# A Hymba-style decoder step: the down products in Strassen's form, the FFN in two phases, and PSUM read in bank pairs

## The chip, the cores and the metric

The kernel runs on one core of a Trainium2 chip. The metric is the device time of one execution in microseconds (us). TensorE (PE) multiplies; a matmul takes a 128x128 block of weights and up to 512 columns of a right operand and accumulates in PSUM, eight banks of 512 float32 columns for each of 128 partitions. VectorE (DVE) and ScalarE (ACT) work on SBUF and PSUM, GpSimd (POOL) on small things, and SyncE (SP) issues nearly all the transfers, in the order of the program, to 16 DMA engines.

## The reference

One decoder layer over 1048 tokens (16 meta tokens, 1024 of a prompt, 8 samples), width 1024. It is a macaron: a half FFN, a mixer (an HGRN2 group and a Mamba-2 group side by side), and a second half FFN.

```python
D_FF = 2816
def swiglu(x, wg, wu, wd):
    return (jax.nn.silu(x @ wg) * (x @ wu)) @ wd

h = h + 0.5 * swiglu(rmsnorm(h, n1), w1g, w1u, w1d)
u = rmsnorm(h, nm) @ w_in
...                                  # HGRN2 and Mamba-2, both with a state
h = h + mix                          # concat(o_hg, yz) @ w_out
h = h + 0.5 * swiglu(rmsnorm(h, n2), w2g, w2u, w2d)
```

All is float32. Besides the 1032 output rows, the states of both groups and of the convolution are returned.

## The kernel before, in words

Activations lie transposed: a tile holds 128 features by T = 1048 tokens, and Q = T/4 = 262 tokens are a quarter. A float32 product is made of three matmuls (`mm3`, L129): each operand is split into a rounded high part (`nc.scalar.copy` into float32r on ScalarE, L126) and the rest (a subtraction on VectorE, L127), and high by high, high by low and low by high are summed in PSUM.

An FFN takes the 2816 hidden features in 22 blocks `f` of 128. `pair` (L300) computes gate and up of one block together as a 2x2 block product in the Strassen-Winograd form: 7 products where the plain form has 8. Its left operands are four pieces of weights and four sums of them (`sum_`, L317, on VectorE), its right operands four blocks of the normed input and four sums, already split and resident in 28 tiles. Each of the 7 products is done for two column halves c, four chunks of the inner dimension and three matmuls each: 14 steps of 12 matmuls of 262 columns. After a step, one operation reads its PSUM bank (L390 to L404); the products come in the order 1, 6, 2, 5, 7, 3, 4, where 2, 3 and 4 add to the banks of 1, 5 and 7. At the end the hidden block silu(g)·u is formed (L409) and split.

`down` (L418) multiplies by the down weights in the plain form. The 22 blocks make six groups of 3 or 4. One pair after a group is complete, its down product is done: 8 output blocks `o` by 4 quarters, 3n matmuls each into a bank of its own, then `h += 0.5·ps` on VectorE (L449). The residual h lies in DRAM in half tiles; it is loaded before and stored after each group (L439, L451). The last group goes quarter by quarter, so that the next norm or the final rows can start on finished quarters.

The order inside an FFN is written out by hand. `Steps` (L275) holds the TensorE steps; `S.before(i, fn)` puts loads, sums and splits ahead of step i. PE, DVE, ACT and SP execute exactly in the order so written. In a pair, weights are asked for 10 and 9 steps ahead, their sums are made 7 to 5 steps ahead, and their splits from 4 steps ahead, one every second step. Outside the FFNs a scheduler orders the work; it may put mixer work between the last steps of the first FFN.

PSUM has two pools of four banks: `acc` for pairs and the mixer's products, `mis` for down products, transposes and norms. SBUF has 30 large slots with the tag `u` and 8 with the tag `s`, nine half tiles `t`, eight weight pieces `r`, and six split weights `ws`.

Of the kernel before, what the change touches and what calls it, by code (L numbers as in the profile page):

```python
# [17 lines left out]
P = 128  # L18
# [46 lines left out]
class Core:  # L65
    def __init__(self, ctx, tc):
# [7 lines left out]
        self.acc = ent(tc.tile_pool(name="acc", bufs=4, space=PSUM))  # L74
# [3 lines left out]
        self.n = 0  # L78

# [15 lines left out]

    def psum(self):
        return self.acc.tile([P, 512], F32, tag="acc", name=self.uid("acc"))
# [202 lines left out]
def pair(K, S, wg, wu, f, ops, first=None):  # L300
# [7 lines left out]
    w, raw, ps, tm, gu, hid = {}, {}, {}, {}, {}, []  # L308

    def load(p, src, k0):  # L310
        raw[p] = K.raw()
        nc.sync.dma_start(raw[p].rearrange("p (k c) -> p k c", k=4), src[:, k0 : k0 + 4, fs])

    def sum_(p, x, y, op):
        if p not in raw:
            raw[p] = K.raw()
        nc.vector.tensor_tensor(raw[p], raw[x], raw[y], op)  # L317

    def split(p):
        w[p] = K.split_w(raw[p])  # L320

    loads = [lambda: load(1, wg, 0), lambda: load(7, wu, 0), lambda: load(4, wu, 4), lambda: load(2, wg, 4)]
    sums = [
        lambda: sum_(5, 7, 4, ALU.add),
        lambda: sum_(6, 5, 1, ALU.subtract),
        lambda: sum_(7, 1, 7, ALU.subtract),
        lambda: sum_(3, 2, 6, ALU.subtract),
    ]
    if first:
        order, blocks, between = first  # L330
        for fn in loads:
            fn()

        def weights():
            for fn in sums:
                fn()
            for p in ORDER[:6]:
                split(p)

        if order == "w":  # L340
            weights()
        blocks(0)
        ops[0].sums()
        for p in ORDER[:2] if order == "w" else ORDER:
            ops[0].split(p)
        if order == "x":
            weights()
        else:
            for i, p in enumerate(ORDER[2:]):
                S.before(s0 + i, lambda p=p: ops[0].split(p))  # L350
        S.before(s0 + 4, lambda: blocks(1))
        S.before(s0 + 4, ops[1].sums)
        S.before(s0 + 6, between)
        for i, p in enumerate(ORDER):
            S.before(s0 + 6 + max(0, i - 1), lambda p=p: ops[1].split(p))
        S.before(s0 + 9, lambda: split(4))
    else:
        for fn, d in zip(loads, (-10, -10, -9, -9)):
            S.before(s0 + d, fn)
        for fn, d in zip(sums, (-7, -7, -6, -5)):  # L360
            S.before(s0 + d, fn)
        for i, p in enumerate(ORDER):
            S.before(s0 + 2 * i - (4 if f > 1 else 3), lambda p=p: split(p))

    def product(p, c):
        if p in (1, 6, 5, 7):
            ps[p, c] = K.psum()[:, :Q]
        more = p in (2, 3, 4)
        if more:
            ps[p, c] = ps[{2: 1, 3: 5, 4: 7}[p], c]  # L370
        wp = w[p]
        hi, lo = ops[c].op[p]
        for k in range(4):
            K.mm3(ps[p, c], wp[:, k * P : k * P + P], wp[:, 512 + k * P : 512 + k * P + P], hi[:, k * Q : k * Q + Q], lo[:, k * Q : k * Q + Q], not more and k == 0, k == 3, more)

    def temp(n, c):
        if n not in tm:
            tm[n] = K.t(2 * Q)
        return tm[n][:, c * Q : c * Q + Q]

    def out(i, q):

        if (i, q // 2) not in gu:
            gu[i, q // 2] = K.t(2 * Q)
        return gu[i, q // 2][:, (q % 2) * Q : (q % 2) * Q + Q]

    def post(p, c):
        b = ps[p, c]
        if p == 1:
            nc.scalar.copy(temp("z", c), b)  # L390
        elif p == 6:
            nc.vector.tensor_add(temp("v", c), b, temp("z", c))
        elif p == 2:
            nc.scalar.activation(out(0, 2 * c), b, AF.Silu)  # L394
        elif p == 5:
            nc.vector.tensor_add(temp("x", c), b, temp("v", c))
        elif p == 7:
            nc.vector.tensor_add(out(1, 2 * c + 1), b, temp("x", c))
        elif p == 3:
            g = out(0, 2 * c + 1)  # L400
            nc.vector.tensor_add(g, b, temp("v", c))  # L401
            nc.scalar.activation(g, g, AF.Silu)  # L402
        else:
            nc.vector.tensor_add(out(1, 2 * c), b, temp("v", c))  # L404
            cs = slice(2 * c * Q, 2 * c * Q + 2 * Q)
            if c == 0:
                hid.extend(K.slot("s" if f % 5 else "u", T, F32R) for i in range(2))
            g, u = gu[0, c], gu[1, c]
            nc.vector.tensor_mul(g, g, u)  # L409
            K.split(g, hid[0][:, cs], hid[1][:, cs])  # L410

    for p, c in [(p, c) for ps_ in (ORDER[:6], ORDER[6:]) for c in range(2) for p in ps_] if first else [(p, c) for p in ORDER for c in range(2)]:
        S.add(lambda p=p, c=c: product(p, c), lambda p=p, c=c: post(p, c))
    return hid
# [1016 lines left out]
```

## Time and profile before

| what | value |
|---|---|
| three runs | 2208.37, 2211.03, 2211.6 us; median 2211.03 |
| profiled execution | 2207.17 us, span 2205.5 us, mean granted clock 0.975 |
| TensorE busy | 2077.0 us (94%), 16078 matmuls |
| VectorE / ScalarE busy | 1306.7 us (59%) / 745.8 us (34%) |
| DMA | 239.40 MB, 35.4% of 16 engines on SP's queue |
| first FFN | about 80 to 815 us |
| second FFN | about 1465 us to the end |

The span runs from the first to the last instruction. TensorE's busy time is the union of its matmuls, which overlap; the distance from start to start is shorter than a duration. The granted clock is the share of full speed that TensorE was given. The table of stretches gives the busy time of each engine and the number of its instructions (x) between two times, then the granted clock, the mean busy share of the DMA engines and the GB/s that they moved. The share can stand above 1.00, since packets overlap. In a group of instructions "out<-in" names tiles, and the last part gives the idle time before them and what ended most of it. In the order of time, square brackets hold the idle time of the engine before an instruction and what ended it.

### The profile page before, as it was taken

The numbers are of one execution on the slowest core, as the hardware profiler recorded it, in microseconds if no ns is written. First come the engines' busy times: TensorE is split into PE (matmuls) and PEld (weight loads), VectorE is DVE, ScalarE is ACT, GpSimd is POOL, SyncE is SP. The second block draws the span as 40 slices with busy tenths as digits, with TensorE's granted clock in tenths as the row PEclk, the third lists the DMA queues.
The fourth block names the chain that finished last, engine by engine and source line by source line (L and its number), as shares of the span: only waits on it lengthen the run. The fifth ranks groups of instructions, "written<-read, shape, count | busy, mean of one in ns | idle before, by whom it ended". The sixth has DMA issues, their size and how long they took to land.

```text
span 2205.5 us, 39636 instructions
## 1 busy us (share of the span) xinstructions
PE 2077.0 (94%) x16078; PEld 2032.7 (92%) x16078; DVE 1306.7 (59%) x2576; ACT 745.8 (34%) x1475; POOL 137.4 (6%) x175
## 2 busy tenths in 40 slices
PE   3899999999999989989999999969999999999996
PEld 3899999999999879978989988969999999999996
DVE  5655646465564586588554457876564655646465
ACT  6422313132231353464523435543131322313122
POOL 1000000000000130141011011300000000000000
PEclk9999999999999999989999999989999999999999
DMA  3425161523516521163022053221625244262542
GB/s 118 107 84 170 54 200 47 171 89 104 154 54 200 156 100 36 55 184 95 36 69 76 4 170 123 86 71 53 198 59 176 73 120 133 59 198 59 175 137 92
DMA packets 276829, 239.40 MB, mean 109 GB/s; under 512 B 18656, under 2 KB 221664, under 8 KB 276640
## 3 DMA queue, kind: packets, MB, share of 16 engines
q1 hardware_dynamic: 275832, 234.73, 35.4%
q8 instruction: 127, 2.08, 0.4%
q10 hardware_dynamic: 592, 2.10, 0.3%
q14 instruction: 54, 0.44, 0.1%
q0 software_dynamic: 224, 0.04, 0.0%
HBM read 169.81 MB, written 67.08 MB: 107 GB/s over the span
## 4 chain that ended last, share of the span: by engine, by line
PE 47%; DVE 5%; ACT 1%; issue 1%; DMA 1%; POOL 0%; SPq 0%; DVEq 0%; ACTq 0%; POOLq 0%
PE acc L134 10%; PE acc L132 10%; PE acc L133 10%; PE mis L132 4%; PE mis L133 3%; PE mis L134 3%; PE mis L1115 2%; DVE s L1129 1%; DVE u L127 1%; PE mis L1154 0%; ACT u L1247 0%; DVE ws L127 0%; DVE u L1253 0%; PE mis L1172 0%; PE mis L1210 0%
## 5 line engine op out<-in xcount | busy, mean ns | idle before, releaser
L132 PE MATMUL acc<-u,ws 128*128 128x262 f32 (+2 forms) x3392 | 1001.5, 295 | 21.3 <-ACT u L126 17.7
L133 PE MATMUL acc<-u,ws 128*128 128x262 f32 (+2 forms) x3392 | 998.5, 294 | 12.1 <-DVE u L127 11.8
L134 PE MATMUL acc<-u,ws 128*128 128x262 f32 (+2 forms) x3392 | 997.5, 294 | 0.0
L132 PEld LDWEIGHTS acc<-u,ws 128*128 128x128 f32 x3392 | 645.9, 190 | 24.3 <-ACT u L126 18.2
L133 PEld LDWEIGHTS acc<-u,ws 128*128 128x128 f32 x3392 | 647.9, 191 | 16.3 <-DVE u L127 14.5
L134 PEld LDWEIGHTS acc<-u,ws 128*128 128x128 f32 x3392 | 645.2, 190 | 0.4
L127 DVE TENSOR_TENSOR ws<-r,ws 128x512 fp32r<-128x512 f32 (+1 forms) x484 | 329.9, 685 | 241.9 <-ACT ws L126 241.3
L126 ACT CAST ws<-r 128x512 fp32r<-128x512 f32 (+1 forms) x484 | 280.6, 613 | 391.7 <-DMA r<-in_w_ffn_down_dram 256.8
L132 PE MATMUL mis<-s,ws 128*128 128x262 f32 x1024 | 293.7, 287 | 2.2 <-DVE u L449 1.3
L133 PE MATMUL mis<-s,ws 128*128 128x262 f32 x1024 | 292.4, 286 | 0.7 <-DVE s L127 0.7
L134 PE MATMUL mis<-s,ws 128*128 128x262 f32 x1024 | 292.2, 285 | 0.0
L449 DVE SCALAR_TENSOR_TENSOR t<-mis,t 128x262 f32<-128x262 f32 x320 | 132.8, 428 | 156.9 <-PE mis L134 156.4
L132 PEld LDWEIGHTS mis<-s,ws 128*128 128x128 f32 x1024 | 195.0, 190 | 3.3 <-DVE u L449 1.7
L133 PEld LDWEIGHTS mis<-s,ws 128*128 128x128 f32 x1024 | 194.9, 190 | 1.3 <-DVE s L127 1.1
L134 PEld LDWEIGHTS mis<-s,ws 128*128 128x128 f32 x1024 | 194.7, 190 | 0.0
L402 ACT ACTIVATE t<-t 128x262 f32<-128x262 f32 x88 | 37.2, 423 | 315.4 <-DVE t L401 315.4
L317 DVE TENSOR_TENSOR r<-r,r 128x512 f32<-128x512 f32 x176 | 121.4, 691 | 37.1 <-DMA r<-in_w_ffn_up_dram 35.6
L132 PE MATMUL mis<-u,ws 128*128 128x262 f32 x288 | 83.1, 289 | 6.8 <-DVE t L449 6.8
L126 ACT CAST s<-t 128x524 fp32r<-128x524 f32 x68 | 42.9, 631 | 126.7 <-DVE t L409 126.7
L133 PE MATMUL mis<-u,ws 128*128 128x262 f32 x288 | 82.6, 287 | 0.0
L134 PE MATMUL mis<-u,ws 128*128 128x262 f32 x288 | 82.6, 287 | 0.0
L394 ACT ACTIVATE t<-acc 128x262 f32<-128x262 f32 x88 | 34.3, 390 | 132.5 <-PE acc L134 132.5
(353 smaller groups left out, 2101.3 us busy)
## 6 DMA issues: line engine op xcount, KB each, us to landing
hd<-t SPq DMA_DIRECT2D x160, 262.0 KB
t<-hd SPq DMA_DIRECT2D x144, 262.0 KB
r<-in_w_ffn_gate_dram SPq DMA_DIRECT2D x88, 256.0 KB
r<-in_w_ffn_up_dram SPq DMA_DIRECT2D x88, 256.0 KB
r<-in_w_ffn_down_dram SPq DMA_DIRECT2D x64, 256.0 KB
r<-in_w_in_dram SPq DMA_DIRECT2D x56, 256.0 KB
u<-hd SPq DMA_DIRECT2D x32, 262.0 KB
r<-in_w_out_dram SPq DMA_DIRECT2D x32, 256.0 KB
```

The source lines that it names most:

```text
L126: self.nc.scalar.copy(hi, src)
L127: self.nc.vector.tensor_sub(lo, src, hi.bitcast(F32))
L132: mm(ps, whi, xhi, start=first, stop=False, skip_group_check=more)
L133: mm(ps, whi, xlo, start=False, stop=False, skip_group_check=more)
L134: mm(ps, wlo, xhi, start=False, stop=last, skip_group_check=more)
L317: nc.vector.tensor_tensor(raw[p], raw[x], raw[y], op)
L394: nc.scalar.activation(out(0, 2 * c), b, AF.Silu)
L402: nc.scalar.activation(g, g, AF.Silu)
L449: nc.vector.scalar_tensor_tensor(t, ps, 0.5, t, ALU.mult, ALU.add)
L1115: nc.tensor.matmul(ps[:, 64 * c : 64 * c + 64], kg[:, P * c : P * (c + 1)], qv[:, c, :, 1], start=True, stop=True)
L1129: nc.vector.tensor_mul(fn, fv[:, :, 0], fv[:, :, 1])
```

## The change

- `down` becomes a Strassen-Winograd product too. A unit j takes two output blocks (2j, 2j+1) and n pairs of hidden blocks: 7 products by 2 column halves, each n chunks by three matmuls, 14 steps of 3n matmuls. The weights of a unit are n·128-column pieces and their four sums, as in `pair`; both use the new `left`, with the same leads.
- The right operands of down are the four blocks of a pair of hidden blocks and four differences of them, each split. `Hidden.jobs` makes them while the next pairs run and stores each of the 7, both parts together, to DRAM.
- The FFN has two phases: first all 22 pairs, then all down units, in three groups of 3, 4 and 4 pairs of hidden blocks, four units each. `Hidden.load` loads a group's 14 operands (7 products by 2 halves, two parts each) into the large slots; they stay for its four units.
- h goes through DRAM as whole tiles, loaded by each unit four steps ahead and stored two steps after, except in the last group, which keeps it.
- PSUM: `acc` has two tiles of two banks. `Unit.both` puts the two halves of a product into one pair, and one instruction reads both (524 columns). `psum()` of the mixer hands out halves of a pair.
- The last unit goes half by half, and the next norm or the final rows start after its first half.

```diff
-        self.acc = ent(tc.tile_pool(name="acc", bufs=4, space=PSUM))
+        self.acc = ent(tc.tile_pool(name="acc", bufs=2, space=PSUM))
...
+    def psum2(self):
+        self.half = None
+        return self.acc.tile([P, 2, 512], F32, tag="acc", name=self.uid("acc"))
...
+    if at:
+        for fns, ds in zip((loads, sums, splits), at):
+            for fn, d in zip(fns, ds):
+                S.before(s0 + d, fn)
+        return w
...
+LEADS = (-10, -10, -9, -9), (-7, -7, -6, -5), [2 * i - 4 for i in range(7)]
...
+class Unit:
+    def bank(self, p, cs, mis):
+        b = {2: 1, 3: 5, 4: 7}.get(p, p)
+        if (b, cs) not in self.ps:
+            K = self.K
+            if len(cs) == 2:
+                self.ps[b, cs] = K.psum2()[:, :, :Q]
...
+    def step(self, S, p, c, cs, mis=False):
+        def mm():
+            new = p in (1, 6, 5, 7)
+            b = self.bank(p, cs, mis)
+            product(self.K, b[:, cs.index(c)], self.w[p], self.ops[c][p], self.n, new, True)
+
+        S.add(mm, (lambda: self.post(p, slice(cs[0], cs[-1] + 1), self.bank(p, cs, mis))) if c == cs[-1] else None)
+
+    def both(self, S):
+        for p in ORDER:
+            for c in range(2):
+                self.step(S, p, c, (0, 1))
...
+class Hidden:
+    GROUPS = (3, 4, 4)
...
+        def split(p, w):
+            self.n += 1
+            st = K.slot("s" if last or self.n % 5 in (0, 2, 4) else "u", T, F32R)
+            hi, lo = st[:, : 2 * Q], st[:, 2 * Q :]
+            K.split(val(p), hi, lo)
+            S.before(w, lambda: nc.sync.dma_start(self.d[g, p][:, :, j, :], st.bitcast(F32).rearrange("p (a t) -> p a t", a=4)))
...
+        at(e0 + 1, sub, 5, 12, 1)
+        for k, p in ((3, 1), (5, 5)):
+            at(e0 + k, split, p, e0 + k + 2)
+        ks = range(1, 9) if last else range(1, 17, 2)
+        for k, (fn, *args) in zip(ks, ((sub, 6, 3, 5), (split, 2), (sub, 7, 3, 12), (split, 3), (split, 6), (sub, 4, 2, 6), (split, 7), (split, 4))):
+            at(e1 + k, fn, *args, *((e1 + k + 2,) if fn is split else ()))
+
+    def load(self, S, g, s0, lead, tags):
...
+        def get(p, c, tag):
+            ops[c][p] = []
+            for part in range(2):
+                t = K.slot(tag, n * Q, F32R)
+                K.nc.sync.dma_start(t.bitcast(F32), self.d[g, p][:, 2 * part + c].rearrange("p n t -> p (n t)"))
+                ops[c][p].append(t)
+
+        for i, (p, c) in enumerate((p, c) for p in ORDER for c in range(2)):
+            S.before(s0 + i - min(lead, 13 + i if tags[i] == "u" else 99), lambda p=p, c=c, i=i: get(p, c, tags[i]))
+        return ops
...
+def down(K, S, wdv, n, f0, j, ops, src, dst=None, h=None, then=None):
...
+    def post(p, cs, b):
+        h11, h12, h21, h22 = (hs[i][:, cs, k] for i in range(2) for k in range(2))
+
+        def acc(t):
+            nc.vector.scalar_tensor_tensor(t, b, 0.5, t, ALU.mult, ALU.add)
+
+        if p == 1:
+            nc.scalar.activation(temp("z", cs), b, AF.Identity, scale=0.5)
+        elif p == 6:
+            nc.vector.scalar_tensor_tensor(temp("v", cs), b, 0.5, temp("z", cs), ALU.mult, ALU.add)
+        elif p == 2:
+            acc(h11)
+            v = temp("v", cs)
+            nc.vector.tensor_add(h12, h12, v)
+            nc.vector.tensor_add(hs[1][:, cs], hs[1][:, cs], v[:, :, None, :].broadcast_to([P, cs.stop - cs.start, 2, Q]))
         else:
+            acc({5: h22, 7: h22, 3: h12, 4: h21}[p])
+        if p == 4 and then:
+            then(2 * j, cs)
+
+    S.before(s0 - 4, load_h)
+    if last:
+        at = [-12, -12, -11, -11], (-9, -9, -8, -7), [-6, -5, -4, -3, -2, 0, 2]
     else:
+        at = LEADS
...
+    if dst:
+        S.before(len(S.steps) + 2, store_h)
...
+        hidden = Hidden(K)
+        for i in range(NF // 2):
+            hid, e = [], []
+            for f in (2 * i, 2 * i + 1):
+                hid.append([])
+                pair(K, S, wgv, wuv, f, ops, hid[-1], first if f == 0 else None)
+                e.append(len(S.steps))
+            hidden.jobs(S, i, hid, *e)
...
+        for g, n in enumerate(Hidden.GROUPS):
+            s0 = len(S.steps)
+            end = g == len(Hidden.GROUPS) - 1
+            gops = hidden.load(S, g, s0, (13, 14, 16)[g], ["u"] * 12 + ["s" if g == 1 else "u"] * 2)
+            then = after(S, h, s0 + 14 * 3 + 7, s0 + 14 * 4) if end else None
+            for j in range(KT // 2):
+                down(K, S, wdv, n, f0, j, gops, (lambda o: hd[o]) if g else src, None if end else lambda o: hd[o], h if end else None, then)
+            f0 += 2 * n
...
+        for q in range(2):
+            S.before(e0 + 2, lambda q=q: nm.end(q))
+            S.before(e0 + 3, lambda q=q: x_mix(q))
+        S.before(e0 + 3, lambda: spill(0))
+        for i in range(3, 7):
+            S.before(e0 + i, lambda: some(3))
+        for q in (2, 3):
+            S.before(e1, lambda q=q: nm.end(q))
+            S.before(e1, lambda q=q: x_mix(q))
+        S.before(e1, lambda: some(99))
...
+        S.before(e0, norm_w)
+        for i in range(9):
+            S.before(e0 + 2 + i if i < 4 else e1, lambda i=i: final(K, a, o, h, nf[0], K.slot("u", D), i))
```

350 lines of the change are left out of this document (171 added, 179 removed).

## The prediction

> **What bounds the kernel now.** I read the page's busy times first, then a table of stretches, then the waits and the order in time where TensorE pauses, and last the groups of VectorE work by shape.
>
> ```profile
> span 2205.5 us, 39636 instructions
> ...
> PE 2077.0 (94%) x16078; PEld 2032.7 (92%) x16078; DVE 1306.7 (59%) x2576; ACT 745.8 (34%) x1475; POOL 137.4 (6%) x175
> ```
>
> TensorE is busy 94% of the span, so a removed matmul is worth its full pitch wherever nothing else becomes late. The stretches below (start:end, length, PE, PEld, DVE, ACT, POOL busy, granted clock, share of the DMA engines, GB/s) show the pitch and the transfer rates.
>
> ```profile
> 160.00:180.00 20.00, 20.00 (x166) 19.95 (x165) 8.79 (x22) 2.05 (x4) 0.00 (x0) 1.00 0.95 303
> 180.00:200.00 20.00, 17.01 (x128) 16.81 (x127) 9.90 (x20) 4.46 (x9) 0.00 (x0) 0.91 0.65 201
> 480.00:500.00 20.00, 20.00 (x167) 20.00 (x166) 13.15 (x25) 6.62 (x16) 0.00 (x0) 1.00 0.19 54
> 755.00:757.50 2.50, 0.00 (x0) 0.00 (x0) 1.13 (x6) 0.97 (x3) 0.00 (x0) 0.93 1.12 305
> 10.00:12.00 2.00, 0.37 (x1) 0.18 (x1) 0.07 (x1) 2.00 (x5) 1.18 (x6) 1.00 1.03 405
> 1315.00:1317.50 2.50, 2.50 (x18) 2.50 (x17) 0.00 (x0) 2.49 (x5) 0.00 (x0) 1.00 1.02 417
> 200.00:300.00 100.00, 100.00 (x823) 100.00 (x822) 58.40 (x112) 28.20 (x58) 0.00 (x0) 1.00 0.31 89
> ```
>
> 823 matmuls in 100 us is a pitch of 0.1214 us (their 0.29 us durations overlap). Rows of 4 KB move at 405 to 417 GB/s with the DMA engines full; weights in 512-byte pieces at 53 to 54 GB/s for a share of 0.19, so about 290. From 160 to 200 the first down products meet a DMA share of 0.95, and 39 matmuls are missing. The waits of 150 to 200 and the order in time say why:
>
> ```profile
> DVE r L317 <- DMA r<-in_w_ffn_up_dram: 3.3, 1, 3.3
> PE mis L132 <- DVE t L449: 3.3, 2, 3.0
> ```
>
> ```profile
> 185.47 0.69 DVE L317 TENSOR_TENSOR r<-r,r 128x512 f32<-128x512 f32 x1 [3.26 <-DMA r<-in_w_ffn_up_dram]
> ```
>
> ```profile
> 187.28 0.59 PE L132 MATMUL mis<-u,ws 128*128 128x262 f32 x1 [2.99 <-DVE t L449]
> 187.67 0.42 PE L133 MATMUL mis<-u,ws 128*128 128x262 f32 x1
> ```
>
> A weight load stands behind other transfers, VectorE stands at the sum of weights (L317) that needs it, the PSUM read queued behind that sum (L449) is late, and TensorE waits 2.99 us and then runs at half pace (0.42 us each) for 2.9 us. This small chain is what I follow into the change.
>
> ```profile
> L317 DVE TENSOR_TENSOR r<-r,r 128x512 f32<-128x512 f32 x176 | 121.4, 691 | 37.1 <-DMA r<-in_w_ffn_up_dram 35.6
> L409 DVE TENSOR_TENSOR t<-t,t 128x524 f32<-128x524 f32 x88 | 62.0, 704 | 3.7
> L127 DVE TENSOR_TENSOR u<-u,u 128x1048 fp32r<-128x1048 f32 x32 | 42.0, 1324 | 21.9 <-ACT u L126 21.9
> L127 DVE TENSOR_TENSOR ws<-r,ws 128x384 fp32r<-128x384 f32 x24 | 13.3, 555 | 23.0 <-ACT ws L126 23.0
> L1253 DVE SCALAR_TENSOR_TENSOR u<-mis,ssq,u 128x512 f32<-128x512 f32 x16 | 11.3, 746 | 0.9
> ```
>
> **The change part by part.** *Matmuls.* Down was 22·8·4·3 = 2112 an FFN; in Strassen's form 11·4·14·3 = 1848. Two FFNs lose 528, at 0.1214 us: **−64.1 us**, if TensorE stays fed.
>
> *Phase one (the 22 pairs, 168 matmuls = 20.4 us each).* VectorE per pair: 11 weight operations at 0.69 (7.6), five PSUM reads of 524 columns, two products at 0.70 (1.4), and half of 4 differences and 7 splits at 0.70 (3.9). A double-bank read is not in the trace: bounds 0.70 (L409) and 0.86 (two of 0.43); I take 0.75, nearest to L1253. That is 16.6 of 20.4 us. Each PSUM read has two products (2.9 us) until its banks are wanted, so I cost it at nothing. ScalarE has about 9 us. The seven operand stores (0.54 MB each) per two pairs add 92 GB/s to 54: hidden. The waits of the old first down blocks go: 39 matmuls at 160 to 200 and 41 at 1560 to 1600: **−9.7 us**.
>
> *Phase two: the six starts of a group.* This decides. A group of n pairs of f has four units of 14 products (3n matmuls: 1.09 us for n = 3, 1.46 for n = 4). Its 14 right operands are all read in unit 0 and stay for all four, so a slot frees only when the last unit of the group before has used it: operand i can be asked for 13 to 16 products before its own. Sizes at 405 and 290 GB/s: an operand 1.07 MB, 2.65 us (n = 3: 0.81 MB, 2.0); two h tiles in or out 1.07 MB, 2.65; a unit's four weights 1.05 MB, 3.6 (n = 3: 2.7); a hidden store 0.54 MB in 1 KB rows, 1.85 (between 1.3 at 405 and 2.0 at the 274 of 512-byte rows); I take the pace of the nearest, the weights. All go through SP in program order, and the instruction order of the changed kernel has them so: weights of unit 0 after operands 0 to 5 (third group: 0 to 6) and a pair of h stores; weights of unit 1 after all operands. VectorE has the next unit's sums ahead of its read of product 5, and product 3 (step 10 of a unit) needs that read. SP issues some 46 transfers at a start; its h loads take a median of 0.42 us each, 19 us of 52, so it is not the limit. TensorE halts at step 10 until the next weights land, plus 1.4 + 0.75 = 2.2 us.
> - Second group (first wait): 6·2.65 + 2.65 + 3.6 = 22.2 us of queue from the first request; TensorE arrives after 9·1.09 = 9.8. Until the weights of unit 1: 14·2.65 + three h transfers 7.95 + two weights 7.2 = 52.3, +2.2; TensorE needs it after 13·1.09 + 10·1.46 = 28.7. Lost in all 25.7.
> - Third group: the same 54.5 against 23·1.46 = 33.5: 21.0.
> - First group: 28.0 + five hidden stores 9.3 + h 2.65 + weights 5.4 + 1.85 = 47.2 against 13·1.46 + 10·1.09 = 29.9: 17.3.
>
> 64.0 an FFN, **+128 us**. From below: at 418 GB/s for everything the second start needs 20.3 MB, 48.6 us, still 22. From above: at the 303 of 160 to 180 it is 67 us, and all six cost 78 us more.
>
> The Trainium skill, "DMA: Bandwidth & Descriptors", section "Specifications", gives one core about 358 GB/s of memory bandwidth; the trace does not agree (405 to 417). By that figure, an estimate, the 4 KB transfers would add about 32 us to the six starts and the time would be near 2311.
>
> *Half pace after a wait.* 2.9 us at 187, longer elsewhere; at 0.217 instead of 0.121 us a matmul the row's 2.9 us lose 1.3, and 5.8 us at 758 lose 2.6. Only the last wait of a start counts: 6·1.9, **+11 us** (0 to 16).
>
> *VectorE in phase two.* n = 4: 7.6 + reads 6·0.75 + an add 0.70 + an add of 1048 columns (0.70 to 1.32; I take 1.3) = 14.1 of 20.4 us: hidden. n = 3: after product 2, 0.75 + 0.7 + 1.3, a split and two sums (0.55 each) end 1.1 us after step 10: three units in two FFNs 7 us. The very last unit goes half by half with one product between read and reuse. Together **+8 us** (0 to 20).
>
> *Ends.* FFN 1 to the mixer: 747.0 to 822, its TensorE idle and half pace some 19 us; afterwards the norms of quarters 2 and 3 and the last 6 operand jobs of quarter 1 stand behind the last matmul (my count 12 to 16). FFN 2: 2139.3 to 2205.5 holds 34.9 us of matmuls, 31 us overhead; afterwards four finals beside the last products and five behind (28). **−6 us** (−20 to +15). In the mixer PSUM has two pairs for four banks; a 350-column product is 3.9 us and its copy 0.45: nothing (to +15, if both halves are held).
>
> *Sum.* 2205.5 − 64.1 − 9.7 + 128 + 11 + 8 − 6 = 2273 span. The profiled execution took 2207.2 (1.7 around its span), the median of the three runs 2211.0, 3.9 more: **2278 us**.
>
> **Rivals.**
> - *The operands are there in time* (the other side). Place: the six starts; it needs 20.3 MB in about 31 us, 650 GB/s; no row is over 418. For it: long stretches at a share of 0.19 leave room, but slots are not free then. Time 2278 − 128 − 11 = 2139. The sign turns where a start costs 12 us with its half pace. Chance 0.08.
> - *Weights do not stand behind operands* (transfers share the engines). Then only the operands' own arrival counts, 46.0 against 33.1 and 37.9, 40.8 against 33.2: 28.5 an FFN; 2278 − 71 = 2207. The 3.26 us wait of L317 speaks against it. Chance 0.08.
> - *Mixed traffic is slower*, 303 as at 160 to 180, where pieces were smaller: 2278 + 78 = 2356. For it: every start mixes reads, stores and weights; against it: three quarters of its bytes are 4 KB rows. Chance 0.12. By the 358 GB/s of the Trainium skill's page the time would lie between this case and mine.
> - *VectorE becomes the bound in phase one*: one us late per pair, 44 us, 2322. For it: four sums, a weight split, two hidden splits and two reads (6.3 us) fall on products 7 to 9 (4.4 us), so a read can slip by 1.9 of its 2.9 us. Chance 0.07.
>
> **How the numbers follow.** My case has 0.65; its own range, from the bounds above, is 2235 to 2325. From 2205 to 2335 leaves out the first rival, most of the third and my case's tails: about 0.2. A difference under 0.2% (4.4 us) can't be told here. The second rival lies on the bound and is shared out (0.03, 0.03, 0.02), and my case keeps 0.01 each for faster and same. Faster: 0.08 + 0.03 + 0.01 = 0.12; same 0.03 + 0.01 = 0.04; slower the rest, 0.84.
>
> **What would show it.** About 353 MB moved; six stretches of 40 to 55 us with the DMA share near 1 and close to 400 GB/s; VectorE's sums of down weights released by DMA, 10 us and more each, twice a start; TensorE's clock dips there and nowhere else in the FFNs; phase one at 823 matmuls per 100 us. Wrong would be: no wait of the sums at the starts, or gaps in phase one.

## The result, and the profile after

The changed kernel takes 2303.01 us (median of 4 runs, 2297.2 to 2304.3) against 2209.7 us before: a ratio of **1.0422, with a 95% interval of 1.0394 to 1.045**. It is slower, by 25 us more than the 2278 us forecast and inside the range of 2205 to 2335. From here on "less" or "more" than the changed kernel is the difference of two such ratios to the kernel before, times 2209.7 us, because each group of experiments had its own runs of the kernel before (medians of 2209.3 to 2213.3 us).

The page of the changed kernel, its span, busy times and DMA packets:

```profile
span 2295.5 us, 38684 instructions
...
PE 2040.8 (89%) x15550; PEld 1982.3 (86%) x15550; DVE 1456.7 (63%) x2516; ACT 799.2 (35%) x1511; POOL 137.1 (6%) x175
...
DMA packets 344315, 353.11 MB, mean 154 GB/s; under 512 B 19584, under 2 KB 301440, under 8 KB 344128
```

528 matmuls are gone, as the change says, and TensorE's share fell from 94% to 89%: more than the work saved has come back as waiting. The bytes moved grew from 239 to 353 MB. The table of stretches (start:end, length, PE, PEld, DVE, ACT, POOL busy, granted clock, share of the DMA engines, GB/s) shows where:

```profile
300.00:400.00 100.00, 100.00 (x825) 100.00 (x824) 72.71 (x115) 35.06 (x65) 0.00 (x0) 1.00 0.52 156
520.00:540.00 20.00, 15.90 (x116) 15.94 (x117) 13.42 (x23) 5.42 (x11) 0.00 (x0) 0.83 1.05 388
540.00:560.00 20.00, 10.39 (x63) 10.21 (x63) 9.63 (x18) 2.48 (x5) 0.00 (x0) 0.66 1.04 351
600.00:620.00 20.00, 5.01 (x34) 4.83 (x33) 5.86 (x10) 1.75 (x3) 0.00 (x0) 0.66 1.04 371
620.00:640.00 20.00, 19.74 (x149) 19.52 (x148) 8.63 (x13) 2.67 (x5) 0.00 (x0) 0.91 1.03 408
700.00:720.00 20.00, 10.86 (x90) 10.64 (x88) 5.17 (x7) 2.49 (x5) 0.00 (x0) 0.89 1.04 364
```

Phase one (300 to 400) is dense: 825 matmuls in 100 us, as many as before. At the three group starts of the first feed-forward (near 525, 605 and 710) the DMA engines are full, at 351 to 408 GB/s, TensorE issues as few as 34 matmuls in 20 us, and its granted clock dips to 0.66. Then the waits of VectorE, and the order in time at the second start (start, duration, engine, line; in brackets the idle time before the instruction and its releaser):

```profile
DVE r L325 <- DMA r<-in_w_ffn_down_dram: 108.1, 12, 14.1
```

```profile
602.86 0.28 PE L145 MATMUL acc<-u,ws 128*128 128x262 f32 x1
...
615.95 1.42 DVE L325 TENSOR_TENSOR r<-r,r 128x512 f32<-128x512 f32 x2 [14.11 <-DMA r<-in_w_ffn_down_dram]
617.28 0.70 DVE L570 SCALAR_TENSOR_TENSOR s<-acc,s 128x524 f32<-128x524 f32 x1
...
618.12 0.56 PE L143 MATMUL acc<-u,ws 128*128 128x262 f32 x1 [14.99 <-ACT ws L137]
618.48 0.42 PE L144 MATMUL acc<-u,ws 128*128 128x262 f32 x1
```

VectorE stands 14.11 us at the sum of down weights (L325). Behind it is the read of a PSUM bank (L570) at 617.28; TensorE's next product starts 0.14 us after that read ends. The profile names a cast of ScalarE as TensorE's releaser, but by its place the halt is the read's: counted in matmuls, all six halts of the first feed-forward stand exactly ahead of step 10, three in the last unit before a group (the last pair, for the first) and three in the first unit of a group. Each of the twelve waits of the sums, 108.1 us, ends some 2 us before one of TensorE's twelve halts (one by one the two lengths differ by up to 2.6 us; the totals agree): in the first feed-forward 6.19 + 9.61, 14.99 + 8.16 and 11.55 + 3.42, in the second 5.42 + 9.31, 14.60 + 9.84 and 12.12 + 2.94, together 108.2 us. Behind ten of the halts, those of 5.42 us and more, 13 to 28 matmuls start every 0.22 us (618.48 and on) instead of every 0.1214, over 3.0 to 6.2 us and at a granted clock of 0.5. Behind the two shortest, 3.42 and 2.94 us, the pace is back with the second matmul and the clock stays at 1.00, though in the kernel before a wait of 2.99 us had half pace behind it (at 187), so the length of a halt alone does not decide:

```profile
748.07 0.36 PE L143 MATMUL acc<-u,ws 128*128 128x262 f32 x1 [3.42 <-issue]
748.27 0.28 PE L144 MATMUL acc<-u,ws 128*128 128x262 f32 x1
748.39 0.28 PE L145 MATMUL acc<-u,ws 128*128 128x262 f32 x1
```

Where the 90 us between the two spans are, with TensorE's excess over 0.1214 us a 262-column matmul (0.158 for the 350-column ones) worked out stretch by stretch from the two traces:

| part | us |
|---|---|
| 528 matmuls fewer | −64.1 |
| waits of the old first down blocks (6.7 and 7.8 us of excess) | −14.5 |
| the six group starts and the rest of phase two (68.0 and 68.4 us of excess, of it 108.2 halts) | +136.4 |
| output projection of the mixer (excess 1.5 us before, 14.6 after) | +13.1 |
| ends of the two feed-forwards (1.2 and 9.1) and the projections behind the first (2.4) | +12.7 |
| head of the kernel, first pairs, rest of the mixer | +6.5 |
| sum | +90.1 |

### The profile page after: what moved, and what is told of

Same layout as the page of the kernel before. It is cut to its first block, busy times and chain, and to the rows that moved or that the text cites. A ratio compares the mean times of both kernels' runs of the same rounds, so it can differ in the third digit from the quotient of the medians.

```text
span 2295.5 us, 38684 instructions
## 1 busy us (share of the span) xinstructions
PE 2040.8 (89%) x15550; PEld 1982.3 (86%) x15550; DVE 1456.7 (63%) x2516; ACT 799.2 (35%) x1511; POOL 137.1 (6%) x175
## 2 busy tenths in 40 slices
DMA packets 344315, 353.11 MB, mean 154 GB/s; under 512 B 19584, under 2 KB 301440, under 8 KB 344128
## 4 chain that ended last, share of the span: by engine, by line
PE 45%; DVE 5%; DMA 4%; ACT 1%; issue 1%; SPq 0%; POOL 0%; DVEq 0%; ACTq 0%; POOLq 0%
PE acc L143 14%; PE acc L144 13%; PE acc L145 13%; DMA r<-in_w_ffn_down_dram 2%; PE mis L1234 2%; DMA u<-hd 1%; DVE r L325 0%; DVE u L1372 0%; PE mis L1273 0%; DVE s L1351 0%; DVE u L138 0%; DVE ws L138 0%; DVE u L253 0%; PE mis L1291 0%; PE mis L1329 0%
## 5 line engine op out<-in xcount | busy, mean ns | idle before, releaser
L143 PE MATMUL acc<-u,ws 128*128 128x262 f32 (+2 forms) x4512 | 1335.8, 297 | 162.1 <-ACT ws L137 74.2
L144 PE MATMUL acc<-u,ws 128*128 128x262 f32 (+2 forms) x4512 | 1324.6, 294 | 13.8 <-DVE u L138 10.7
L145 PE MATMUL acc<-u,ws 128*128 128x262 f32 (+2 forms) x4512 | 1322.1, 294 | 0.0
L143 PEld LDWEIGHTS acc<-u,ws 128*128 128x128 f32 x4512 | 866.1, 192 | 182.9 <-ACT ws L137 78.7
L144 PEld LDWEIGHTS acc<-u,ws 128*128 128x128 f32 x4512 | 870.9, 193 | 16.3 <-DVE u L138 12.2
L145 PEld LDWEIGHTS acc<-u,ws 128*128 128x128 f32 x4512 | 866.2, 192 | 0.4
L138 DVE TENSOR_TENSOR ws<-r,ws 128x512 fp32r<-128x512 f32 (+1 forms) x562 | 380.2, 680 | 252.7 <-ACT ws L137 251.7
L137 ACT CAST ws<-r 128x512 fp32r<-128x512 f32 (+1 forms) x562 | 325.4, 606 | 337.2 <-DMA r<-in_w_ffn_down_dram 126.7
L325 DVE TENSOR_TENSOR r<-r,r 128x512 f32<-128x512 f32 (+1 forms) x272 | 181.1, 679 | 126.8 <-DMA r<-in_w_ffn_down_dram 108.1
L570 DVE SCALAR_TENSOR_TENSOR s<-acc,s 128x524 f32<-128x524 f32 (+1 forms) x120 | 78.6, 655 | 87.0 <-PE acc L145 86.1
L202 POOL TENSOR_TENSOR t<-t,t 128x262 f32<-128x262 f32 x56 | 48.5, 877 | 889.6 <-ACT t L201 888.9
L138 DVE TENSOR_TENSOR s<-s,s 128x524 fp32r<-128x524 f32 x98 | 68.4, 698 | 0.4 <-ACT s L137 0.4
L137 ACT CAST s<-s 128x524 fp32r<-128x524 f32 x98 | 61.7, 630 | 8.9 <-DVE s L503 8.9
L428 DVE TENSOR_TENSOR s<-t,t 128x524 f32<-128x524 f32 (+1 forms) x92 | 58.5, 677 | 1.6
L138 DVE TENSOR_TENSOR u<-u,u 128x1048 fp32r<-128x1048 f32 x32 | 41.5, 1311 | 26.7 <-ACT u L137 26.7
```

The lines of the kernel that those rows point to most:

```text
L137: self.nc.scalar.copy(hi, src)
L138: self.nc.vector.tensor_sub(lo, src, hi.bitcast(F32))
L143: mm(ps, whi, xhi, start=first, stop=False, skip_group_check=more)
L144: mm(ps, whi, xlo, start=False, stop=False, skip_group_check=more)
L145: mm(ps, wlo, xhi, start=False, stop=last, skip_group_check=more)
L202: K.nc.gpsimd.tensor_add(self.sq[q], self.sq[q], t)
```

## Experiments

My theory was that of the prediction: at a group start more bytes are asked for than two units of work can cover; the weights stand behind operands in SP's queue; VectorE has sums that wait for those weights ahead of a PSUM read that TensorE needs. Rivals: VectorE or the PSUM pairs halt TensorE whatever the transfers do; or the bytes alone do it, and the order of queues is no matter.

**Half the operand bytes.**

```diff
-            for part in range(2):
-                t = K.slot(tag, n * Q, F32R)
-                K.nc.sync.dma_start(t.bitcast(F32), self.d[g, p][:, 2 * part + c].rearrange("p n t -> p (n t)"))
-                ops[c][p].append(t)
+            t = K.slot(tag, n * Q, F32R)
+            K.nc.sync.dma_start(t.bitcast(F32), self.d[g, p][:, c].rearrange("p n t -> p (n t)"))
+            ops[c][p] = [t, t]
```

> The changed kernel, but each right operand is loaded with its high part alone, and the high part stands in for the low one (the products lack the low part's correction, and use the high part twice). TensorE, VectorE and ScalarE issue the same work, but 7.5 MB less are loaded in each of the six group starts, which moved about 20 MB. Theory (the transfers of a group start are more than the two units can cover, so TensorE's halts of 53.9 and 54.2 us and the half pace behind them are transfer time): some 12.8 MB at 405 GB/s are 32 us, less than the 41 us from the first issue to the end of unit 0, so nearly all of the 108 us of halts goes, with the half pace after them: 90 to 125 us less than the changed kernel's 2303, 2178 to 2213. Rival A (VectorE's order of sums and reads, or the PSUM pairs, halts TensorE, whatever the transfers do): at most 20 us less, 2283 to 2303. Rival B (the weights' own 512-byte rows set the halts, the operands only stand beside them): halts of at least 50 us stay, 2240 or more.

Measured: 2203.27 us, ratio 0.9982 (0.9967 to 0.9997), 97 us less than the changed kernel. The page has 311.77 MB instead of 353.11; 41.3 MB at the 405 GB/s of the prediction's row are 102 us. The second start, in its stretches:

```profile
575.00:595.00 20.00, 15.33 (x126) 15.14 (x125) 11.30 (x19) 3.61 (x8) 0.00 (x0) 0.94 0.84 293
595.00:615.00 20.00, 20.00 (x148) 20.00 (x149) 11.77 (x19) 3.69 (x7) 0.00 (x0) 0.89 1.00 366
```

Four fifths of the halts are gone (TensorE's pauses over 0.4 us in phase two are 22 us in both feed-forwards together, against 110) with the same work on TensorE, VectorE and ScalarE: without these transfers the halts hardly arise. Both rivals of this run fall. The run also fills half as many large slots, so its loads wait less for a free one; the run with unsplit operands, below, fills as many as the changed kernel and gains nearly as much, so the bytes are the larger part.

**The weights on ScalarE's queue.**

```diff
-        nc.sync.dma_start(raw[p].rearrange("p (k c) -> p k c", k=n), src)
+        (dma or nc.sync.dma_start)(raw[p].rearrange("p (k c) -> p k c", k=n), src)
...
-    w = left(K, S, s0, srcs, n, at, (lambda: K.slot("u", 1024, F32R)) if last else None)
+    w = left(K, S, s0, srcs, n, at, (lambda: K.slot("u", 1024, F32R)) if last else None, nc.scalar.dma_start)
```

> The changed kernel, complete, with the loads of the down weights issued by ScalarE on a queue of their own; the right operands stay with SyncE. Theory in its two parts. The bytes: about 18 MB must land by step 13 of unit 0, 45 us at 405 GB/s where some 38 us of work cover them, so at least 8 us of halts a start stay, 48 us in all. The order: the rest of the 108 us is weights that stand behind operands which are needed later, and goes. Together 30 to 60 us less, 2243 to 2273. Rival A (order alone, the bytes would fit): under 30 us of halts stay, 2190 to 2220. Rival B (bytes alone): the halts move from the weights to the operands and stay at 100 us or more, 2290 to 2310, and the waits name the operands' loads instead of the weights'.

Measured: 2307.02 us, ratio 1.0446 (1.0426 to 1.0466): no gain; rival B's number, but not its waits: the sums still wait for weights, half as long, and the reads now wait for h tiles.

```profile
DVE r L325 <- DMA r<-in_w_ffn_down_dram: 57.5, 18, 7.8
DVE s L570 <- DMA s<-hd: 52.1, 5, 13.5
```

The order in time at the second start, first of this kernel, then of the changed kernel (ACTq and SPq issue the loads, x is how many):

```profile
592.95 0.61 ACT L573 ACTIVATE t<-acc 128x524 f32<-128x524 f32 x1 [8.12 <-PE acc L145]
593.39 0.37 ACTq L320 DMA_DIRECT2D r<-in_w_ffn_down_dram  x1
...
593.86 2.85 ACTq L320 DMA_DIRECT2D r<-in_w_ffn_down_dram  x3
...
608.25 1.42 DVE L325 TENSOR_TENSOR r<-r,r 128x512 f32<-128x512 f32 x2 [7.84 <-DMA r<-in_w_ffn_down_dram]
```

```profile
601.16 2.05 SPq L320 DMA_DIRECT2D r<-in_w_ffn_down_dram  x2
606.95 2.80 SPq L320 DMA_DIRECT2D r<-in_w_ffn_down_dram  x2
```

The weights were asked for at 593.4 to 596.7 instead of 601.2 to 609.8, and VectorE's sum ran at 608.25 instead of 615.95. But the load that the sum needs took 12 us or more from its request (9.0 in the changed kernel, 606.95 to 615.95), and the issue itself stands behind ScalarE's wait for TensorE (8.12 us). TensorE's waits of phase two in the first feed-forward (505 to 752, pauses over 0.4 us) are 47.9 us against 55.0, spread over more places, with more slow matmuls behind them. So this run alone did not settle whether the order matters, and I come back to it below. The Trainium skill, "DMA: Bandwidth & Descriptors", section "Issuing engines are not separate DMA queues", says that transfers started by different engines share the same DMA engines, and that a second issuer saves only the time of issuing; this run (2307.02 against 2303.01 us) agrees.

**One group without a start.**

```diff
-            gops = hidden.load(S, g, s0, (13, 14, 16)[g], ["u"] * 12 + ["s" if g == 1 else "u"] * 2)
+            if g < 2:
+                gops = hidden.load(S, g, s0, (13, 14)[g], ["u"] * 14)
```

> The changed kernel, but the third group multiplies its weights with the second group's operands, which stay where they are: the third group's own operands are not loaded, and its products are not the reference's. Theory (a group start has a price of its own): two of the six starts go, with halts of 11.55 + 3.42 and 12.12 + 2.94 us, 30 us, and 2 to 4 us of half pace behind each: 32 to 40 us less, 2263 to 2271. Rival A (the halts belong to the units' own chain of weights, sums and splits and come with any change of group): no change, within 8 us of 2303. Rival B (phase two as a whole is short of transfer time): the other starts shrink too, more than 45 us less.

Measured: 2267.89 us, ratio 1.0277 (1.0258 to 1.0297), 32 us less. Where the third start was, the stretch is dense:

```profile
700.00:720.00 20.00, 20.00 (x166) 20.00 (x166) 12.69 (x19) 3.94 (x9) 0.00 (x0) 1.00 0.47 156
```

A third start costs 16 us, and the units behind it nothing: the other two starts kept their halts (14.7 and 23.1 us in the first feed-forward). Phase two with its operands in place is as dense as phase one, so VectorE is no limit in the units of four pairs.

**The output projection's banks.**

```diff
-                ps = K.psum()[:, :Q]
+                ps = K.psm()[:, :Q]
```

> The changed kernel, complete; the output projection takes single banks of the other PSUM pool (four of them) instead of halves of the two bank pairs. From its first to its last addition it took 95.9 us before and 106.4 us after, with TensorE waiting 6.9 us for the additions. Theory (two pairs instead of four banks leave TensorE less room ahead of VectorE's queue): the stretch goes back to 95 to 98 us and the kernel takes 8 to 11 us less, 2292 to 2295. Rival A (the stretch is longer because of what the change put on VectorE and ScalarE beside it): the stretch stays at 104 us or more and the time within 3 us of 2303. Rival B (the other pool's own users, the norms, now collide): longer than 2303.

Measured: 2296.94 us, ratio 1.0401 (1.0383 to 1.0419), 4.6 us less; the two intervals overlap, so the stretch in the trace is the better witness. From first to last addition it took 99.6 us, against 106.4 in the changed kernel. This line of the changed kernel's waits in that stretch has no like in the run's:

```profile
PE acc L143 <- DVE s L1351: 6.9, 15, 1.2
```

Two pairs give TensorE less room ahead of VectorE than four single banks. Most of the loss comes back (6.8 of 10.5 us); 3.7 us of the stretch do not.

**VectorE's sums.** Two runs take the sums of weights out of the way of the reads: on GpSimd, or later in VectorE's own order.

```diff
-        nc.vector.tensor_tensor(raw[p], raw[x], raw[y], op)
+        (add or nc.vector.tensor_tensor)(raw[p], raw[x], raw[y], op)
...
+    w = left(K, S, s0, srcs, n, at, (lambda: K.slot("u", 1024, F32R)) if last else None, nc.gpsimd.tensor_tensor)
```

> The changed kernel, complete, with the four sums of each block of down weights on GpSimd instead of VectorE: no sum that waits for weights stands ahead of VectorE's reads of the banks. Theory (the bytes of a start set the halts; VectorE's order only decides at which step TensorE stops): the halts move to where the weights' casts are needed and the time stays within 8 us of 2303, 2295 to 2311. Rival (VectorE's order turns late weights into halts that would else be hidden): the halts of a start shrink by a third or more, 30 us or more less, 2273 or below.

Measured: 2274.39 us, ratio 1.0277 (1.0254 to 1.03), 32 us less: the rival's number; the theory as I had put it there falls. It had read too much into the first run: that bytes make the weights late does not make VectorE's order harmless. The second run moves the sums later on VectorE itself.

```diff
-        at = LEADS
+        at = LEADS[0], (-3, -3, 3, 5), LEADS[2]
```

> The changed kernel, complete, with the sums of the down weights late: two at step -3 and two at steps 3 and 5 of the block instead of -7 to -5. VectorE does the same work; only its order is changed. Sums on GpSimd took 2274.39 with the kernel before at 2213.28, some 33 us less than the changed kernel. Theory (it was the order: reads of the banks behind sums that wait for weights): 15 to 35 us less than 2303, 2268 to 2288. Rival (it was the work taken from VectorE, or GpSimd running ahead with sums as soon as weights land): within 8 us of 2303.

Measured: 2267.73 us, ratio 1.0263 (1.0239 to 1.0287), 35 us less, with the same instructions on each engine. The waits of the sums:

```profile
DVE r L325 <- DMA r<-in_w_ffn_down_dram: 24.3, 12, 4.2
```

108.1 us became 24.3, and TensorE now pauses mostly where a unit begins (10.31 us at step 0 of the second group's first unit), no longer at step 10. In this kernel, with all its bytes, a third of what the starts cost is VectorE's order.

**The weights on GpSimd's queue.** The edit for ScalarE's queue, with another issuer.

```diff
-    w = left(K, S, s0, srcs, n, at, (lambda: K.slot("u", 1024, F32R)) if last else None)
+    w = left(K, S, s0, srcs, n, at, (lambda: K.slot("u", 1024, F32R)) if last else None, nc.gpsimd.dma_start)
```

> The changed kernel, complete, with the down weights' loads issued by GpSimd, which has nothing else to do in phase two: they stand behind no operand, and unlike those that ScalarE issued (2307.02) behind no work of the issuing engine either, only behind a free buffer. Theory (the weights are late because they stand behind operands in one queue; VectorE's sums then hold the reads): the weights' waits go, VectorE's order no longer matters, and the gain is about that of the late sums (2267.73) or more, 2240 to 2275; what is left is operands, since the bytes stay. Rival A (the bytes alone make the weights late, from whichever queue): within 10 us of 2303. Rival B (GpSimd issues a load so slowly that the weights come later still): 2315 or more.

Measured: 2264.68 us, ratio 1.0258 (1.0217 to 1.03), 36 us less; the theory's number. GpSimd asked for the next weights at 581.21 and on, not at 601.16, and VectorE's longest wait for weights at the second start fell from 14.11 to 4.00 us. What is late next, in the order in time:

```profile
581.21 0.77 POOL L320 DMA_DIRECT2D r<-in_w_ffn_down_dram  x1 [9.64 <-DVE ws L138]
...
596.37 0.75 POOL L320 DMA_DIRECT2D r<-in_w_ffn_down_dram  x1 [7.10 <-issue]
...
603.26 0.69 DVE L325 TENSOR_TENSOR r<-r,r 128x512 f32<-128x512 f32 x1 [4.00 <-DMA r<-in_w_ffn_down_dram]
...
612.84 1.62 SPq L552 DMA_DIRECT2D s<-hd  x2
...
625.25 0.70 DVE L570 SCALAR_TENSOR_TENSOR s<-acc,s 128x524 f32<-128x524 f32 x1 [8.22 <-issue]
```

A free buffer held the first of these loads, but not most of those behind it: from 584.90 on GpSimd asked for nearly every one 0.30 us after the load before it had landed, beside the operands some 7 us apart (588.51, 596.37, 603.47, 610.31). Four weights then take some 27 us, where a unit of four pairs takes 20.4. Why these loads go one at a time was not tested. The h tiles are asked for at 612.84, behind operands in SP's queue, and the add into them is VectorE's next stand; that it waits for their load is read from the order of the queue, the profile says only "issue". So what stands ahead of the weights does matter. ScalarE's run had a second queue too and gained nothing, but there the weights were asked for 2.8 us after the last unit of the first group began, here 3.7 us before it. The two runs together suggest that the early request pays and not the second queue; no run separates them further. Rivals A and B fall. Weights ahead of the operands in SP's own queue were not tried: the eight raw buffers are in use until step 8 of the unit before, when the last of its weights is split.

**A storage with half the bytes.** Operands stored unsplit, as one block, and split after the load; complete results.

```diff
-                self.d[g, p] = K.dram.tile([P, 4, n, Q], F32, name=K.uid("hd"))
+                self.d[g, p] = K.dram.tile([P, 2, n, Q], F32, name=K.uid("hd"))
...
+            S.before(w, lambda: nc.sync.dma_start(self.d[g, p][:, :, j, :], val(p).rearrange("p (a t) -> p a t", a=2)))
...
+            hi, lo = K.slot(tag, n * Q, F32R), K.slot(tag, n * Q, F32R)
+            K.nc.sync.dma_start(lo.bitcast(F32), self.d[g, p][:, c].rearrange("p n t -> p (n t)"))
+            ops[c][p] = [hi, lo]
+        def cut(p, c):
+            hi, lo = ops[c][p]
+            K.split(lo.bitcast(F32), hi, lo)
...
+            S.before(s0 - 10 + 20 * i // 13, lambda p=p, c=c: cut(p, c))
```

> The changed kernel, complete, but the right operands lie in DRAM unsplit, as one fp32 block each, and are split into their two parts after they are loaded. A start loads 7.5 MB less, as in the run with the high parts alone, which took 2203.27 us; phase one stores half as much and loses its splits. In exchange VectorE takes 14 subtractions more at each start, of 1.31 us each (the 128x1048 row), 18.3 us. Phase two keeps VectorE busy for 0.61 of the time (12.23 of 20 us at 660), so the some 35 us into which the splits are spread have 13.7 us free. Theory (bytes make the halts, and VectorE has the room but for 4.6 us a start): 2203 plus up to 28 us, 2203 to 2231. Rival A (VectorE takes it all in its idle time): 2195 to 2205. Rival B (the subtractions stand ahead of VectorE's reads and hold TensorE by their full time, 110 us in six starts): 2290 or more.

Measured: 2214.29 us, ratio 1.0007 (0.9994 to 1.002), 92 us less than the changed kernel. That is 5 us over the run with the high parts alone (0.9982), within the theory's bounds.

**Part of the new subtractions on GpSimd**, on top of that.

```diff
         def cut(p, c):
             hi, lo = ops[c][p]
-            K.split(lo.bitcast(F32), hi, lo)
+            if ORDER.index(p) % 3 == 2:
+                K.nc.scalar.copy(hi, lo.bitcast(F32))
+                K.nc.gpsimd.tensor_sub(lo, lo.bitcast(F32), hi.bitcast(F32))
+            else:
+                K.split(lo.bitcast(F32), hi, lo)
```

> As the run with operands unsplit in DRAM, but GpSimd does 4 of the 14 subtractions of a start (0.877 us for 128x262 in the page, so about 3.5 us each, 14 us in the start). VectorE's share is 13.1 us, within the 13.7 us that it has free. Theory (VectorE's queue is what is left at the starts): 5 to 25 us less than the unsplit kernel. Rival A (VectorE wasn't short): within 5 us of it. Rival B (the slower engine's results come late, and TensorE waits for them): more than 5 us longer.

Measured: 2243.89 us, ratio 1.0145 (1.0118 to 1.0171), 30 us more than with all subtractions on VectorE: rival B's direction. But VectorE's own instructions became slower, which I had not written. The same two sums of weights on VectorE at the second start, first all on VectorE, then beside GpSimd:

```profile
590.95 1.42 DVE L325 TENSOR_TENSOR r<-r,r 128x512 f32<-128x512 f32 x2 [1.45 <-DMA r<-in_w_ffn_down_dram]
```

```profile
594.15 3.88 DVE L325 TENSOR_TENSOR r<-r,r 128x512 f32<-128x512 f32 x2 [1.71 <-DMA r<-in_w_ffn_down_dram]
```

The pair takes 3.88 us instead of 1.42, while GpSimd subtracts, and TensorE's halt behind it, at step 10 of that unit, is 7.31 us instead of 4.59. At the third start an add of two SBUF tiles takes 3.51 us for 1.24 and a subtraction 2.88 for 0.68, and the halt is 5.71 us for 1.23. TensorE's pauses of phase two in the first feed-forward are 26 us for 15; more of the cause at the end.

**Unsplit storage and single banks**, the two edits together.

```diff
-                ps = K.psum()[:, :Q]
+                ps = K.psm()[:, :Q]
```

> Operands unsplit in DRAM, with the output projection in single banks of the other PSUM pool, complete. If the two gains lie in different places of the kernel they add: 4 to 9 us less than the unsplit kernel alone (2303.01 less 2296.94 was 6.1). If the unsplit kernel comes out near 2203, this one is near 2197, below the 2209.73 of the kernel before.

Measured: 2208.69 us, ratio 0.9984 (0.997 to 0.9998); 5 us less than the unsplit kernel, as expected if the gains add; the two intervals touch.

**And the weights on ScalarE's queue**, on top of these two.

```diff
-    w = left(K, S, s0, srcs, n, at, (lambda: K.slot("u", 1024, F32R)) if last else None)
+    w = left(K, S, s0, srcs, n, at, (lambda: K.slot("u", 1024, F32R)) if last else None, nc.scalar.dma_start)
```

> Operands unsplit in DRAM, the output projection in single banks (2208.69 us), and the loads of the down weights on ScalarE's own queue. Complete. With the operands in two parts the second queue changed nothing (2307.02 against 2303.01), since the bytes did not fit. Theory (now that they fit, a weight that needn't stand behind operands comes in time): the weights' waits of some 4.6 us at the second start and 1.2 to 2 us elsewhere go, 5 to 15 us less, 2194 to 2204. Rival (the queue is not what makes them late): within 4 us of 2208.69.

Measured: 2263.73 us, ratio 1.0241 (1.0219 to 1.0263): 57 us more, outside both expectations. In the traces the excess lies in phase two of both feed-forwards. At the second start the weights are asked for shortly after ScalarE's read of product 1 in both kernels, but summed 15.4 us after that read here (589.07 to 604.44) and 12.0 us with one queue (581.78 to 593.80). It isn't that SP put more operands beside them: it asked for nine operand loads from 588.04 to 600.38 here, and for nine from 580.72 to 591.47 with one queue. Whether it is the sharing between two queues, or ScalarE's issuing among its casts, was not tested; the cause stays open.

**Or the late sums**, with unsplit storage and single banks, and one queue.

```diff
-        at = LEADS
+        at = LEADS[0], (-3, -3, 3, 5), LEADS[2]
```

> Operands unsplit in DRAM, the output projection in single banks (2208.69 us), and the sums of the down weights late: two at step -3 and two at steps 3 and 5 instead of -7 to -5, each just ahead of the split that needs it. Complete. What is left of halts at the three starts of a feed-forward is about 15 us with some 5 us of slower pace. Theory (VectorE reaches its sums before the weights have landed, and its reads stand behind them): a late weight now holds VectorE 4 to 8 us later, and 5 to 20 us go, 2189 to 2204. Rival (the weights themselves are what is late, the casts wait for them in any case): within 4 us of 2208.69.

Measured: 2200.55 us, ratio **0.9957 (0.994 to 0.9973)**: a little faster than the kernel before, by 0.4%, and the best of all. The interval overlaps a little with that of the kernel without late sums, so this last step is likely, not certain. Its page:

```profile
span 2203.1 us, 38427 instructions
...
PE 2031.3 (92%) x15550; PEld 1972.7 (90%) x15550; DVE 1457.1 (66%) x2446; ACT 796.2 (36%) x1441; POOL 134.4 (6%) x175
...
DMA packets 292792, 270.44 MB, mean 123 GB/s; under 512 B 18240, under 2 KB 260672, under 8 KB 292608
```

## Why the prediction was right, and where it was off

- *Direction and mechanism: right, and shown.* The halts stand at step 10, twice a start, and go when the bytes are halved (−97 us), and in part when the weights are asked for early (−36) or the sums stand later (−35). The last two are two cuts through one chain and do not add to the first. Two of the signs were too strong: of the twelve waits of the sums five are 10 us or more (3.41 to 14.11 in all), and the clock dips in the last unit of a feed-forward too (0.83 from 820 to 840).
- *Matmuls*, −64.1: 528 fewer, as said. *Old waits*: −14.5 for −9.7; 11.0 of it lies in the pairs beside the first down products, where I had counted missing matmuls, and the rest is spread thinly over all pairs.
- *Group starts*, +128: the halts were 108.2 us. The three starts cost 15 to 16, 23 to 24 and 15 us; I had 17.3, 25.7 and 21.0. The third was oversized, by 6. The transfers were no faster than I took them (full stretches at 351 to 408 GB/s), but more were done before the start: six of the 28 operand parts were asked for by 684.42, 13 us before the next one (697.60), where the second start had two:

```profile
680.62 4.12 SPq L532 DMA_DIRECT2D u<-hd  x6
```

```profile
581.55 1.15 SPq L532 DMA_DIRECT2D u<-hd  x2
```

The second group keeps four of its parts in small slots, so four more of the 30 large ones were free. Four parts are two operands, 5.3 us at the price of my sum, which would make up most of the 6.
- *Half pace*, +11, and *VectorE in phase two*, +8: phase two's excess beyond the halts is 136.4 − 108.2 = 28 us, of it some 21 of slow matmuls near the starts (pitches between 0.1214 and 0.7 us). The term that failed is "only the last wait of a start counts: 6·1.9": ten of the twelve halts have slow matmuls behind them, some 2 us of loss each, and at the third start it is the first halt that has them and not the last. VectorE had no share in the units of four, as the run without a third start shows; in the units of three that lie inside a group TensorE pauses 0.5 us at step 10 (four times in all), less than the 7 us I had. Taken together, starts, pace and VectorE came to 136 us against 147. Part of the match in time is luck: these 11 us and the 5 more that the old waits gave back offset some of the 38 us that the mixer, the ends and the first pairs cost beyond the forecast.
- *Mixer*, "nothing (to +15, if both halves are held)": +13.1 us in the output projection, which I had put at nothing. I had priced a 350-column product of 3.9 us; the projection's products are 12 matmuls, 1.5 us, with splits on VectorE between the reads. The run with single banks gave back 6.8 us of the stretch.
- *Ends*, −6 (−20 to +15): +12.7, inside the bounds but on the other side, and with 18.7 us the term that was mis-sized by most. Of it 9.1 us are the second feed-forward's end: behind the last product 20.7 us remain, where the kernel before had 14.5, and last unit and rest together have 40.4 us beside their matmuls, where I had 28. In both feed-forwards VectorE holds the last half unit. In the first TensorE waits 6.34 us for a read that stands behind norms and operand jobs on VectorE, as the order in time of the changed kernel has it:

```profile
823.85 0.43 DVE L228 TENSOR_TENSOR u<-t,u 128x262 fp32r<-128x262 f32 x1
824.20 0.48 DVE L225 SCALAR_TENSOR_TENSOR t<-s,col,t 128x262 f32<-128x262 f32 x1
824.60 0.42 DVE L228 TENSOR_TENSOR u<-t,u 128x262 fp32r<-128x262 f32 x1
824.95 0.42 DVE L570 SCALAR_TENSOR_TENSOR s<-acc,s 128x262 f32<-128x262 f32 x1
...
825.42 0.58 PE L143 MATMUL acc<-u,ws 128*128 128x262 f32 x1 [6.34 <-DVE s L570]
```

That another order there would gain was not tried; VectorE is busy nearly throughout, so it may only move the wait.
- *No term at all* for the head, the first pairs and the rest of the mixer: +6.5 us. The second pair begins at 94.6 us instead of 90.5; why, I did not look.
- *Phase one at nothing*: right, 825 matmuls in 100 us, and a bank-pair read took 0.70 us on VectorE where I had 0.75.
- *Rivals.* "Operands in time" is what the runs with half the bytes come near to, not this kernel. "VectorE bounds phase one" is out by the dense stretch. "Weights do not stand behind operands" described a kernel that the GpSimd run approximates: it gains 36 us where I had priced 71, with its own loads one at a time and new waits that, by the queue's order, are for h tiles. "Mixed traffic at 303 GB/s" is out by 351 to 408. The estimate by the Trainium skill's 358 GB/s, 2311, came nearer to the time than mine, but by chance: the starts ran at up to 408 GB/s, and what I lacked lay in the mixer, the ends and the first pairs.

## What to carry to other kernels

Before an operand is moved to DRAM, divide its bytes by the time between the moment its buffer frees and the moment it is used: here some 20 MB against about 40 us of work cost more than 528 matmuls saved, and storing it in half the bytes, with 14 more subtractions a start, turned the loss into nearly nothing. Then look at what in-order engines have queued behind the late transfer: putting the sums just ahead of their use was worth 35 us without a byte or an instruction saved. A pool of bank pairs should be priced at every user of the old single banks, the shortest products first.

## What the runs showed of the hardware that I had not expected

In these runs VectorE instructions that read two tiles in SBUF slowed down beside GpSimd, and those that read PSUM and one SBUF tile did not. With the sums on GpSimd, VectorE's 128x512 subtractions (L138) took 1.26 us on average when they overlapped one (31 of them) and 0.695 when not, while its reads of bank pairs (L570) took 0.695 beside them and 0.699 elsewhere. With operand subtractions on GpSimd, the 8 that overlapped took 2.48 us. The Trainium skill, "SBUF — State Buffer", section "Who interferes with whom", says so: a VectorE instruction with two SBUF inputs contends with a GpSimd instruction that reads SBUF, since they share a read interface, and one with a single SBUF input, outside VectorE's two-port modes, does not. The traces agree. An idle GpSimd is therefore no free help for VectorE, though it paid for the sums, where it took over the long waits.
